# Attention in a two-layer trunk: the loop over heads turned into a loop over branches, four heads per value matmul

## The chip, the cores and the metric

The kernel runs on one core of a Trainium2 chip. The metric is the device time of one execution in microseconds (us), lower is better. A core has a tensor engine (PE), a vector engine (DVE), a scalar engine (ACT), GpSimd (POOL) and a sync engine (SP) that issues most loads. Each engine works through its own instructions strictly in the order in which they were queued when the program was built. PE writes only into PSUM banks of 128 partitions by 512 float32 values.

## The reference

Two layers, each of a mixer (three branches in parallel: this attention, and two recurrences), a cross attention and a gated feed-forward part, over 512 positions of width 1024. The change lies in the attention of the mixer. Eight query heads of 64 share two groups of keys and values (four heads to a group). Each head's output is a gated sum of three attentions: over compressed keys, over selected blocks, and over a causal window. With 512 positions there are 8 blocks, and all of them are selected, so the last two are plain causal softmax attentions over different keys and values.

```python
s = jnp.einsum('bgqhd,bgqnd->bgqhn', qb, kg).astype(F32) * scale
p = masked_softmax(s, mask)
return jnp.einsum('bgqhn,bgqnd->bgqhd', p.astype(vg.dtype), vg)
...
g = jax.nn.sigmoid(gate_logits.astype(F32)).reshape(B, S, G, HG, 3)
o = g[..., 0:1] * o_cmp + g[..., 1:2] * o_sel + g[..., 2:3] * o_win
```

## The kernel before

All weights are multiplied in a split form: `load_w` loads a float32 tile `wr`, ACT rounds it to `wh`, DVE subtracts to get `wl`, and three matmuls of 512 columns stand for one. A gate projection (`gate(b, n)`) is 24 such matmuls into one bank of the pool `pd`, followed by a multiplication on DVE and a tanh on ACT.

The attention (`nsa_attn`) takes the positions in four blocks `i` of 128 queries. Block `i` attends to `W = 128 (i+1)` keys, so the widths are 128, 256, 384 and 512. A block begins with the compressed branch for all eight heads: eight small matmuls against `kcT`, a chain of a dozen short DVE operations and one exponential, a transpose, and the tile `pc`. Then come 16 softmaxes (8 heads, two branches `br`). For one softmax PE writes the scores into a bank of the pool `pa` (two score matmuls and one that adds the causal mask, `negb`), DVE finds the row maximum (TENSOR_REDUCE) and scales it (a one-column TENSOR_TENSOR), ACT takes the exponential with its row sum (ACTIVATE and ACTIVATION_READ_ACCUMULATOR), which frees the bank. Four softmaxes make a group: one reciprocal of the four sums, one multiplication by the gate, four scalings (TENSOR_SCALAR, L1097), transposes on PE into the pool `pt`, copies from there to SBUF on ACT, and value matmuls from those copies.

Before, a group is one head index `j` with both key groups and both branches. Its output bank `po` comes from `pa`, and its value matmuls have 128 columns.

A scheduler orders each engine's instructions when the program is built: it may bring a later instruction ahead of an earlier one if its operands and its buffer are free by then. In source order the gate projections for the other two branches stand behind the attention, in `mixer`. The pools have these numbers of buffers:

```python
return pp.tile([P, T], F32, tag="pd", name=f"pd_{uid[0]}", bufs=3)
...
return pp.tile([P, T], F32, tag="pa", name=f"pa_{uid[0]}", bufs=2)
...
return pp.tile([P, T], F32, tag="pt", name=f"pt_{uid[0]}", bufs=3)
```

Of the kernel before, what the change touches and what calls it, by code (L numbers as in the profile page):

```python
# [13 lines left out]
AF = mybir.ActivationFunctionType  # L14
# [5 lines left out]
P = 128  # L20
# [68 lines left out]
TOK_VS, TOK_VW, TOK_HI, TOK_G, TOK_B, TOK_A = 0, 128, 256, 512, 536, 540  # L89
# [110 lines left out]
def tile_trunk(ctx, tc, a, out, dbg=None):  # L200
    nc = tc.nc
    dbg = dbg or {}
    V, S, G, TE = nc.vector, nc.scalar, nc.gpsimd, nc.tensor
# [7 lines left out]
    def tl(tag, bufs, shape=(P, T), dt=F32):  # L211
        uid[0] += 1
        return sb.tile(list(shape), dt, tag=tag, name=f"{tag}_{uid[0]}", bufs=bufs)

    def chain():
        return tl("chain", NCHAIN)

    def pd():
        uid[0] += 1
        return pp.tile([P, T], F32, tag="pd", name=f"pd_{uid[0]}", bufs=3)  # L220

    def pa():
        uid[0] += 1
        return pp.tile([P, T], F32, tag="pa", name=f"pa_{uid[0]}", bufs=2)

    def pt():
        uid[0] += 1
        return pp.tile([P, T], F32, tag="pt", name=f"pt_{uid[0]}", bufs=3)

    def small(n, dt=F32):  # L230
        if n <= 16:
            return tl("tiny", 40, (P, 16), dt)[:, :n]
        return tl("small", 10, (P, 64), dt)[:, :n]

    def mm(out_, lhsT, rhs, start=True, stop=True):
        TE.matmul(out_, lhsT, rhs, start=start, stop=stop, skip_group_check=True)  # L236
# [5 lines left out]
    def act(o, i, f=AF.Copy, **kw):  # L242
        S.activation(o, i, f, **kw)  # L243

    def tt(o, x, y, op, eng=None):
        (eng or V).tensor_tensor(o, x, y, op)  # L246

    def ts(o, x, s1, s2, op0, op1=None, eng=None):
        if op1 is None:
            (eng or V).tensor_scalar(o, x, s1, None, op0)  # L250
        else:
            (eng or V).tensor_scalar(o, x, s1, s2, op0, op1)
# [4 lines left out]
    MUL, ADD, SUB, MAX = ALU.mult, ALU.add, ALU.subtract, ALU.max  # L257

    def mark(name):
        if "mark" in dbg:  # L260
            dbg["mark"](name, nc)
# [7 lines left out]
    ident = cm[:, C_ID:C_ID + P]  # L269
# [185 lines left out]
    vcpad = [cst.tile([P, 4, 64], F32, name=f"vcpad{i}") for i in range(2)]  # L455
# [571 lines left out]
    def nsa_attn(l, tok, y, st):  # L1027
        KH, KL, QS, kcT, r8 = (st[k] for k in ("KH", "KL", "QS", "kcT", "r8"))
        mark("attn")
        gall = tl("gall", 1, (P, NT, 24))  # L1030
        act(gall, tok[:, :, TOK_G:TOK_G + 24], AF.Tanh, scale=0.5)
        ts(gall, gall, 0.5, 0.5, MUL, ADD)

        for i in range(NT):
            qs_ = slice(i * P, (i + 1) * P)
            sc = pa()
            for j in range(4):
                for g_ in range(2):
                    mm(sc[:, (4 * g_ + j) * 64:(4 * g_ + j + 1) * 64], QS[j, g_][:, qs_],
                       kcT[:, g_].rearrange("p a n -> p (a n)"))  # L1040
            e = tl("tg", NTG)[:, :256].rearrange("p (h n) -> p h n", h=8)
            m3 = cmpm[:, i:i + 1, :].to_broadcast([P, 8, 32])
            pen = tl("cmpn", 1, (P, 32))
            ts(pen, cmpm[:, i, :], -NEG, NEG, MUL, ADD)
            p3 = pen[:, None, :].to_broadcast([P, 8, 32])
            s4 = sc.rearrange("p (h a n) -> p h a n", a=2, n=32)
            tt(e, s4[:, :, 0], p3, ADD)
            tt(e, e, s4[:, :, 1], ADD)
            b8 = lambda t_, n_=32: t_.rearrange("p (h o) -> p h o", o=1).to_broadcast([P, 8, n_])
            tt(e, e, b8(r8[:, i]), MUL)  # L1050
            mx = small(8)
            V.tensor_reduce(mx, e, AX.X, MAX)
            tt(e, e, b8(mx), SUB)
            act(e, e, AF.Exp)
            tt(e, e, m3, MUL)
            dn = small(8)
            V.tensor_reduce(dn, e, AX.X, ADD)
            ts(dn, dn, 1e-30, None, MAX)
            V.reciprocal(dn, dn)
            g3 = gall[:, i, :].rearrange("p (h b) -> p h b", b=3)  # L1060
            cf = small(8)
            tt(cf, dn, g3[:, :, 0], MUL)
            tt(e, e, b8(cf), MUL)
            ps = pt()
            for g_ in range(2):
                TE.transpose(ps[:, g_ * P:(g_ + 1) * P], e[:, g_ * 4:g_ * 4 + 4, :].rearrange("p h n -> p (h n)"), ident)
            pc = tl("tg", NTG)
            act(pc[:, :256], ps[:, :256])

            for j in range(4):  # L1070
                hd = {}
                W = (i + 1) * P
                WM = max(W, 256)
                den = small(4)
                prs = []
                for g_ in range(2):
                    for br in range(2):
                        q_ = QS[j, g_][:, qs_]
                        ps = pa()
                        mm(ps[:, :WM], q_, KH[br, g_][:, :WM], stop=False)  # L1080
                        mm(ps[:, :WM], q_, KL[br, g_][:, :WM], start=False, stop=False)
                        mm(ps[:, i * P:W], identb, negb, start=False, stop=True)
                        nm = small(1)
                        V.tensor_reduce(nm, ps[:, :W], AX.X, MAX, negate=True)  # L1084
                        rc = r8[:, i, 4 * g_ + j:4 * g_ + j + 1]
                        tt(nm, nm, rc, MUL)
                        pr = chain()
                        act(pr[:, :W], ps[:, :W], AF.Exp, bias=nm, scale=rc, accum_out=den[:, 2 * g_ + br:2 * g_ + br + 1])
                        prs.append(pr)
                V.reciprocal(den, den)  # L1090
                g4 = gall[:, i, :].rearrange("p (g j b) -> p g j b", g=2, b=3)[:, :, j, 1:]
                tt(den.rearrange("p (g b) -> p g b", g=2), den.rearrange("p (g b) -> p g b", g=2), g4, MUL)
                for g_ in range(2):
                    for br in range(2):
                        x_ = 2 * g_ + br
                        pr = prs[x_]
                        ts(pr[:, :W], pr[:, :W], den[:, x_:x_ + 1], None, MUL)  # L1097
                        pst = pt()
                        for k in range(i + 1):
                            TE.transpose(pst[:, k * P:(k + 1) * P], pr[:, k * P:(k + 1) * P], ident)  # L1100
                        pT = chain()
                        act(pT[:, :W], pst[:, :W])
                        hd[g_, br] = pT
                po = pa()
                o_ = [po[g_ * 64:(g_ + 1) * 64, :P] for g_ in range(2)]
                for g_ in range(2):
                    mm(o_[g_], vcpad[g_][:, j, :], pc[:, g_ * P:(g_ + 1) * P], start=True, stop=False)
                for br, off in ((0, TOK_VS), (1, TOK_VW)):
                    for k in range(i + 1):
                        for g_ in range(2):  # L1110
                            mm(o_[g_], tok[:, k, off + g_ * 64:off + g_ * 64 + 64], hd[g_, br][:, k * P:(k + 1) * P],
                               start=False, stop=(br == 1 and k == i))
                act(y[j][:, qs_], po[:, :P])
                yield


    def mem_phase(norm):
# [90 lines left out]
    def mixer(l, norm):  # L1208
# [68 lines left out]
        for _ in nsa_attn(l, tok, ya, st):  # L1277
            pass
# [169 lines left out]
```

## Time and profile before

| what | value |
|---|---|
| median of 3 runs | 2110.07 us (2108.05 to 2112.93) |
| the profiled execution: span, which is all that its profile gives of its own time | 2108.7 us |
| PE matmuls, busy | 2057.5 us, 98% of the span |
| DVE busy | 1430.0 us, 68% |
| ACT busy | 951.3 us, 45% |
| POOL busy | 131.9 us, 6% |

Busy time is the time in which an engine has at least one instruction under way. A matmul's record lasts from its start until its results have landed, and the next one starts before that, so that PE can be busy all the time and still not be at its peak: the distance from start to start tells what a matmul costs. The attention of the first layer runs from 365.7 to 552.7 us of the span and that of the second from 1398.5 to 1586.1 us.

### The profile page before, as it was taken

Reading aid. Unit: us, or ns where it says so; the run is one execution under the profiler, and the core shown is the slowest. Engines: PE = TensorE matmul, PEld = TensorE weight load, DVE = VectorE, ACT = ScalarE, POOL = GpSimd, SP = SyncE. Lnnn points to the kernel's source line nnn. Section 1 sums busy time; section 2 is a strip of 40 time slices with the busy share of each in tenths; the row PEclk is TensorE's granted clock in tenths of the full one; section 3 lists DMA queues with packets and bytes.
Section 4 is the critical chain, followed back from the end, with each engine's and each line's share of the span. In section 5 each row is a group of like instructions: output and inputs, shape, how many; then the busy total and the mean of one; then the engine's idle time right before and its main releaser. Section 6 shows DMA issues by size and latency. Waiting matters only on the chain. (4 is left out here: it accounts for less than half of the span.)

```text
span 2108.7 us, 31046 instructions
## 1 busy us (share of the span) xinstructions
PE 2057.5 (98%) x11396; PEld 1610.2 (76%) x11400; DVE 1430.0 (68%) x3070; ACT 951.3 (45%) x1854; POOL 131.9 (6%) x120
## 2 busy tenths in 40 slices
PE   8999999999999999999999998999999999999999
PEld 7877677777786788888888776777778758888887
DVE  6764898666656887377548469975667577755773
ACT  6434444555545544244434344445554454433442
POOL 1000122000010100000000003110000110000000
PEclk9999999999999999999999999999999999999999
DMA  7332222111241233323432312121113413333333
GB/s 237 90 101 68 77 74 64 52 51 46 64 140 47 88 95 95 95 94 96 120 107 76 101 42 90 59 72 51 46 46 91 126 52 92 95 93 98 95 98 108
DMA packets 116809, 180.90 MB, mean 86 GB/s; under 512 B 19696, under 2 KB 37232, under 8 KB 116656
## 3 DMA queue, kind: packets, MB, share of 16 engines
q1 hardware_dynamic: 88992, 158.64, 25.1%
q10 hardware_dynamic: 27584, 19.97, 3.3%
q8 instruction: 90, 1.47, 0.3%
q14 instruction: 63, 0.52, 0.1%
q0 software_dynamic: 80, 0.29, 0.0%
HBM read 170.21 MB, written 8.65 MB: 85 GB/s over the span
## 5 line engine op out<-in xcount | busy, mean ns | idle before, releaser
L236 PE MATMUL pd<-act,wh 128*128 128x512 f32 x3008 | 985.4, 403 | 0.0
L243 ACT ACTIVATE wh<-wr 128x512 fp32r<-128x512 f32 (+2 forms) x586 | 365.5, 624 | 657.5 <-PE pd L236 566.3
L236 PEld LDWEIGHTS pd<-act,wh 128*128 128x128 f32 x3008 | 560.6, 189 | 128.4 <-issue 14.4
L236 PE MATMUL pd<-act,wl 128*128 128x512 f32 x1504 | 605.6, 403 | 1.4 <-DVE wl L246 1.4
L246 DVE TENSOR_TENSOR wl<-wr,wh 128x512 fp32r<-128x512 f32 (+2 forms) x586 | 406.7, 694 | 212.3 <-ACT wh L243 205.0
L236 PE MATMUL pd<-chain,wh 128*128 128x512 f32 x1344 | 426.7, 397 | 4.4 <-DVE gate L255 3.2
L236 PEld LDWEIGHTS pd<-act,wl 128*128 128x128 f32 x1504 | 284.3, 189 | 69.0 <-issue 6.1
L236 PEld LDWEIGHTS pd<-chain,wh 128*128 128x128 f32 x1344 | 251.0, 188 | 66.0 <-ACT chain L243 3.7
L236 PE MATMUL pd<-chain,wl 128*128 128x512 f32 x672 | 266.4, 396 | 0.3
L246 DVE TENSOR_TENSOR gate<-pd,rb 128x512 f32<-128x512 f32 x168 | 116.0, 691 | 102.8 <-PE pd L236 101.3
L236 PE MATMUL pa<-chain,chain 128*64 128x64 f32 (+7 forms) x1248 | 163.2, 296 | 2.3 <-ACT chain L243 1.0
L236 PEld LDWEIGHTS pd<-chain,wl 128*128 128x128 f32 x672 | 126.6, 188 | 30.3 <-DVE wl L246 1.1
L255 DVE SCALAR_TENSOR_TENSOR gate<-gate,vec,gate 128x511 f32<-128x511 f32 (+1 forms) x176 | 132.1, 751 | 21.5 <-ACT gate L243 18.3
L236 PEld LDWEIGHTS pa<-chain,chain 128*64 128x64 f32 (+3 forms) x1248 | 109.1, 163 | 45.5 <-issue 21.0
L1084 DVE TENSOR_REDUCE tiny<-pa 128x1 f32<-128x128 f32 (+3 forms) x128 | 61.1, 487 | 81.7 <-PE pa L236 81.3
L243 ACT ACTIVATE chain<-pa,tiny,r 128x128 f32<-128x128 f32 (+3 forms) x128 | 78.9, 617 | 60.7 <-DVE tiny L246 56.3
L246 POOL TENSOR_TENSOR chain<-chain,t 128x512 f32<-128x512 f32 x30 | 40.7, 1355 | 1014.7 <-ACT t L243 949.0
L243 ACT ACTIVATE chain<-pt 128x512 f32<-128x512 f32 (+3 forms) x156 | 61.1, 445 | 63.9 <-PE pt L1100 37.2
L243 ACT ACTIVATE gate<-gate,vec 128x512 f32<-128x512 f32 x88 | 63.8, 726 | 27.9 <-DVE gate L246 27.9
L236 PE MATMUL pa<-chain,tok 128*64 128x128 f32 x704 | 62.3, 282 | 0.0
L255 DVE SCALAR_TENSOR_TENSOR t<-t,gate 128x512 f32<-128x512 f32 x88 | 60.5, 688 | 2.0 <-ACT t L243 0.4
L246 POOL TENSOR_TENSOR tg<-tg,chain 128x256 f32<-128x256 f32 (+1 forms) x42 | 45.5, 1089 | 191.1 <-ACT tg L243 78.5
(238 smaller groups left out, 2001.5 us busy)
## 6 DMA issues: line engine op xcount, KB each, us to landing
wr<-in_w_fm SPq DMA_DIRECT2D x184, 256.0 KB, 2.7
wr<-in_w_up SPq DMA_DIRECT2D x176, 256.0 KB, 2.6
wr<-in_w_dn SPq DMA_DIRECT2D x64, 256.0 KB, 2.7
wr<-in_w_mix SPq DMA_DIRECT2D x32, 256.0 KB, 2.7
wr<-in_w_dn SPq DMA_DIRECT2D x32, 192.0 KB, 2.4
wr<-in_w_tk SPq DMA_DIRECT2D x16, 272.0 KB, 2.9
wr<-in_w_kv SPq DMA_DIRECT2D x16, 256.0 KB, 3.8
chain<-in_cmp_w SPq DMA_DIRECT2D x16, 256.0 KB, 4.1
```

Of the source, the lines that this page charges most:

```text
L236: TE.matmul(out_, lhsT, rhs, start=start, stop=stop, skip_group_check=True)
L243: S.activation(o, i, f, **kw)
L246: (eng or V).tensor_tensor(o, x, y, op)
L255: V.scalar_tensor_tensor(o, x, s, y, op0, op1)
L1084: V.tensor_reduce(nm, ps[:, :W], AX.X, MAX, negate=True)
```

## The change

The loop over heads `j` with both branches inside becomes a loop over branches `br`, then key groups `g_`, with the four heads inside. A group of four softmaxes is now one branch of one key group. For each key block `k` the four heads' transposes go side by side into one `pt` bank, one copy of 512 columns takes them to SBUF (`pT[g_, k]`), and one value matmul of 512 columns serves all four heads. The output bank `po` of a whole block, 512 columns wide, now comes from `pd`. It is written first by the eight value matmuls of the compressed branch, collects both branches, and is copied out at the end of the block by four copies, two on ACT and two on DVE.

```diff
+            W = (i + 1) * P
+            WM = max(W, 256)
+            po = pd()
+            o_ = [po[g_ * 64:(g_ + 1) * 64] for g_ in range(2)]
             for j in range(4):
-                hd = {}
-                W = (i + 1) * P
-                WM = max(W, 256)
-                den = small(4)
-                prs = []
                 for g_ in range(2):
-                    for br in range(2):
+                    mm(o_[g_][:, j * P:(j + 1) * P], vcpad[g_][:, j, :], pc[:, g_ * P:(g_ + 1) * P],
+                       start=(j == 0), stop=False)
+            g5 = gall[:, i, :].rearrange("p (g j b) -> p g j b", g=2, b=3)
+            for br, off in ((0, TOK_VS), (1, TOK_VW)):
+                pT = {}
+                for g_ in range(2):
+                    den = small(4)
+                    prs = []
+                    for j in range(4):
                         q_ = QS[j, g_][:, qs_]
...
-                V.reciprocal(den, den)
...
-                        for k in range(i + 1):
-                            TE.transpose(pst[:, k * P:(k + 1) * P], pr[:, k * P:(k + 1) * P], ident)
-                        pT = chain()
-                        act(pT[:, :W], pst[:, :W])
-                        hd[g_, br] = pT
-                po = pa()
...
-                act(y[j][:, qs_], po[:, :P])
+                    V.reciprocal(den, den)
+                    tt(den, den, g5[:, g_, :, 1 + br], MUL)
+                    for j in range(4):
+                        ts(prs[j][:, :W], prs[j][:, :W], den[:, j:j + 1], None, MUL)
+                    for k in range(i + 1):
+                        pst = pt()
+                        for j in range(4):
+                            TE.transpose(pst[:, j * P:(j + 1) * P], prs[j][:, k * P:(k + 1) * P], ident)
+                        pT[g_, k] = chain()
+                        act(pT[g_, k], pst)
+                for k in range(i + 1):
+                    for g_ in range(2):
+                        mm(o_[g_], tok[:, k, off + g_ * 64:off + g_ * 64 + 64], pT[g_, k],
+                           start=False, stop=(br == 1 and k == i))
                 yield
+            for j in range(4):
+                (S.copy if j % 2 else V.tensor_copy)(y[j][:, qs_], po[:, j * P:(j + 1) * P])
+            yield
```

The change also moves instructions on every engine. In the rows below `pd_5236` and the like are banks of `pd`, `act` and `wh`, `wl` the split activations and weights of the projections, `tg` is `pc`, and `chain` stands for queries, keys, probabilities and their transposes.

PE at the start of block 0 of the first layer, before:

```order
L236 MATMUL pa_3876<-chain_2583,chain_3724 128x256
L236 LDWEIGHTS identb
L236 MATMUL pa_3876<-negb,identb 128x128
L236 MATMUL pd_5236<-act_160,wh_5239 128x512
L236 MATMUL pd_5236<-act_161,wh_5239 128x512
L236 MATMUL pd_5236<-act_160,wl_5240 128x512
L236 MATMUL pd_5236<-act_202,wh_5239 128x512
L236 MATMUL pd_5236<-act_203,wh_5239 128x512
L236 MATMUL pd_5236<-act_202,wl_5240 128x512
L236 MATMUL pa_3885<-chain_2594,chain_3724 128x256
```

PE at the same place, with the change:

```order
L236 MATMUL pa_3885<-negb,identb 128x128
L236 MATMUL pa_3894<-chain_2582,chain_3730 128x256
L236 MATMUL pa_3894<-chain_2583,chain_3730 128x256
L236 LDWEIGHTS identb
L236 MATMUL pa_3894<-negb,identb 128x128
L1066 MATMUL pt_3870<-cm,tg_3852 128x128 x2
L236 MATMUL pa_3903<-chain_2582,chain_3736 128x256
L236 MATMUL pa_3903<-chain_2583,chain_3736 128x256
L236 LDWEIGHTS identb
L236 MATMUL pa_3903<-negb,identb 128x128
L236 MATMUL pd_3875<-tg_3873,vcpad_86 64x128
```

The projection matmuls into `pd` no longer stand between the scores. In the whole order of PE the first of them now stands in block 3, after its compressed value matmuls, and four projections (96 matmuls) stand in that block; the others follow the attention.

PE between two groups of block 1, with the change (`pa_4191` and `pa_4200` are the first two scores of the next group, `pa_4209` is its third; `pt_4176` and `pt_4183` are the two transpose banks of the group before):

```order
L236 MATMUL pa_4200<-negb,identb 128x128
L1104 MATMUL pt_4176<-cm,chain_4141 128x128
L1104 MATMUL pt_4183<-cm,chain_4141 128x128
L1104 MATMUL pt_4176<-cm,chain_4150 128x128
L1104 MATMUL pt_4183<-cm,chain_4150 128x128
L1104 MATMUL pt_4176<-cm,chain_4159 128x128
L1104 MATMUL pt_4183<-cm,chain_4159 128x128
L1104 MATMUL pt_4176<-cm,chain_4168 128x128
L1104 MATMUL pt_4183<-cm,chain_4168 128x128
L236 MATMUL pd_4124<-chain_4181,tok_533 64x512
L236 MATMUL pa_4209<-chain_2588,chain_3739 128x256
```

Two scores stand ahead of the transposes, and the third stands behind the transposes and behind a value matmul that needs a copy of them (`chain_4181`).

DVE at such a boundary in block 1, before (`pa_4251` is the next group's first score):

```order
L1090 RECIPROCAL tiny_4175<-tiny_4175 128x4
L246 TENSOR_TENSOR tiny_4175<-tiny_4175,gall_3840 128x4
L246 TENSOR_TENSOR wl_5458<-wr_5455,wh_5457 128x512
L250 TENSOR_SCALAR chain_4183<-chain_4183,tiny_4175 128x256
L250 TENSOR_SCALAR chain_4192<-chain_4192,tiny_4175 128x256
L250 TENSOR_SCALAR chain_4201<-chain_4201,tiny_4175 128x256
L250 TENSOR_SCALAR chain_4210<-chain_4210,tiny_4175 128x256
L1084 TENSOR_REDUCE tiny_4255<-pa_4251 128x1
```

DVE and then ACT at such a boundary in block 1, with the change (`pa_4252` is the first score of the group after, `pt_4176` and `pt_4183` hold the transposes of the group before, `pa_4191` and `pa_4200` are the scores of the next):

```order
L1091 TENSOR_REDUCE tiny_4256<-pa_4252 128x1
L1097 RECIPROCAL tiny_4190<-tiny_4190 128x4
L246 TENSOR_TENSOR tiny_4256<-tiny_4256,r_769_3697 128x1
L246 TENSOR_TENSOR tiny_4190<-tiny_4190,gall_3840 128x4
L250 TENSOR_SCALAR chain_4198<-chain_4198,tiny_4190 128x256
L250 TENSOR_SCALAR chain_4207<-chain_4207,tiny_4190 128x256
L250 TENSOR_SCALAR chain_4216<-chain_4216,tiny_4190 128x256
L250 TENSOR_SCALAR chain_4225<-chain_4225,tiny_4190 128x256
```

```order
L243 ACTIVATE chain_4168,tiny_4133<-pa_4161,tiny_4165,r_769_3697 128x256
L243 ACTIVATE chain_4181<-pt_4176 128x512
L243 ACTIVATE chain_4188<-pt_4183 128x512
L243 ACTIVATE chain_4198,tiny_4190<-pa_4191,tiny_4195,r_769_3697 128x256
L243 ACTIVATE chain_4207,tiny_4190<-pa_4200,tiny_4204,r_769_3697 128x256
```

On DVE the next group's first maximum has moved ahead of the reciprocal. On ACT the copies of a group's transposes stand ahead of the next group's first exponential.

## Rows read from the trace of the kernel before

**Rows 1.** The page: span, busy time of PE, its busy tenths and granted clock.

```profile
span 2108.7 us, 31046 instructions
...
PE 2057.5 (98%) x11396; PEld 1610.2 (76%) x11400; DVE 1430.0 (68%) x3070; ACT 951.3 (45%) x1854; POOL 131.9 (6%) x120
...
PEclk9999999999999999999999999999999999999999
```

**Rows 2.** Busy us (x instructions) by engine in both attentions; granted clock, DMA share, GB/s.

```profile
365.70:552.70 187.00, 187.00 (x1181) 138.06 (x1180) 117.00 (x343) 101.88 (x265) 0.00 (x0) 1.00 0.16 49
1398.50:1586.10 187.60, 187.30 (x1181) 138.00 (x1179) 117.03 (x339) 101.72 (x265) 0.00 (x0) 1.00 0.16 49
```

**Rows 3.** The same windows, instructions on pd alone; then 610 to 630 us.

```profile
365.70:552.70 187.00, 118.85 (x405) 71.68 (x405) 15.11 (x22) 0.00 (x0) 1.00 0.16 49
...
610.00:630.00 20.00, 20.00 (x88) 16.11 (x86) 2.77 (x4) 0.00 (x0) 1.00 0.50 150
```

**Rows 4.** Timeline of PE in block 2: start, duration, instruction.

```profile
457.48 1.62 PE L1100 MATMUL pt<-cm,chain 128*128 128x128 f32 x12
...
459.39 0.50 PE L236 MATMUL pd<-act,wh 128*128 128x512 f32 x1
459.82 1.52 PE L236 MATMUL pa<-chain,tok 128*64 128x128 f32 x22
461.28 0.62 PE L236 MATMUL pa<-chain,chain 128*128 128x384 f32 x2
```

**Rows 5.** Timeline of one softmax of block 3, 512 wide.

```profile
531.72 0.63 PE L236 MATMUL pa<-chain,chain 128*128 128x512 f32 x2
...
532.46 0.69 DVE L1084 TENSOR_REDUCE tiny<-pa 128x1 f32<-128x512 f32 x1 [0.91 <-PE pa L236]
...
533.43 0.78 ACT L243 ACTIVATE chain<-pa,tiny,r 128x512 f32<-128x512 f32 x1 [0.98 <-DVE tiny L246]
...
534.11 0.19 ACT L243 ACTIVATION_READ_ACCUMULATOR chain<-pa,tiny,r 128x1 f32 x1
```

**Rows 6.** Groups in the first attention by line and shape: busy us, mean ns.

```profile
L243 ACT ACTIVATE chain<-pa,tiny,r 128x512 f32<-128x512 f32 x16 | 12.5, 780 | 8.2 <-DVE tiny L246 7.1 <-DVE tiny L1291 1.0
...
L1084 DVE TENSOR_REDUCE tiny<-pa 128x1 f32<-128x512 f32 x16 | 10.7, 687 | 12.3 <-PE pa L236 12.3
...
L243 ACT ACTIVATE chain<-pa,tiny,r 128x128 f32<-128x128 f32 x16 | 7.3, 457 | 6.0 <-DVE tiny L246 4.9 <-PE pa L236 1.0
...
L250 DVE TENSOR_SCALAR chain<-chain,tiny 128x512 f32<-128x512 f32 x16 | 6.7, 480 | 0.1
...
L1084 DVE TENSOR_REDUCE tiny<-pa 128x1 f32<-128x128 f32 x16 | 4.5, 287 | 6.7 <-PE pa L236 6.5
...
L250 DVE TENSOR_SCALAR chain<-chain,tiny 128x128 f32<-128x128 f32 x16 | 3.6, 281 | 0.1
```

**Rows 7.** Timeline of DVE, then of ACT, at the end of a group of block 3.

```profile
534.86 0.17 DVE L1090 RECIPROCAL tiny<-tiny 128x4 f32<-128x4 f32 x1
...
535.14 0.69 DVE L246 TENSOR_TENSOR wl<-wr,wh 128x512 fp32r<-128x512 f32 x1
535.75 1.67 DVE L250 TENSOR_SCALAR chain<-chain,tiny 128x512 f32<-128x512 f32 x4
...
537.13 2.06 ACT L243 ACTIVATE chain<-pt 128x512 f32<-128x512 f32 x4 [1.52 <-PE pt L1100]
```

**Rows 8.** Timeline of DVE at the head of block 3: the compressed branch.

```profile
497.17 0.42 DVE L1052 TENSOR_REDUCE tiny<-tg 128x8 f32<-128x256 f32 x1
...
499.98 0.68 DVE L1084 TENSOR_REDUCE tiny<-pa 128x1 f32<-128x512 f32 x1
```

**Rows 9.** Timeline of PE in the cross attention: float32 matmuls of 512 columns.

```profile
1716.22 1.88 PE L236 MATMUL pa<-chain,chain 128*128 128x512 f32 x4
```

**Rows 10.** Windows in that cross attention, columns as in rows 2.

```profile
1698.80:1702.20 3.40, 2.09 (x8) 0.96 (x7) 3.36 (x17) 2.25 (x7) 0.00 (x0) 0.99 0.27 77
1702.20:1705.60 3.40, 3.40 (x5) 1.32 (x5) 0.09 (x1) 0.00 (x1) 0.00 (x0) 0.50 0.00 0
```

More of the change, by code (lines that the diff above doesn't have):

```diff
@@ L1087, in nsa_attn @@
                         pr = chain()
-                        act(pr[:, :W], ps[:, :W], AF.Exp, bias=nm, scale=rc, accum_out=den[:, 2 * g_ + br:2 * g_ + br + 1])
+                        act(pr[:, :W], ps[:, :W], AF.Exp, bias=nm, scale=rc, accum_out=den[:, j:j + 1])
                         prs.append(pr)
-                V.reciprocal(den, den)
-                g4 = gall[:, i, :].rearrange("p (g j b) -> p g j b", g=2, b=3)[:, :, j, 1:]
-                tt(den.rearrange("p (g b) -> p g b", g=2), den.rearrange("p (g b) -> p g b", g=2), g4, MUL)
@@ L1093, in nsa_attn @@
[L1093 to L1097, printed above, removed]
-                        pst = pt()
-                        for k in range(i + 1):
-                            TE.transpose(pst[:, k * P:(k + 1) * P], pr[:, k * P:(k + 1) * P], ident)
-                        pT = chain()
-                        act(pT[:, :W], pst[:, :W])
-                        hd[g_, br] = pT
@@ L1104, in nsa_attn @@
-                po = pa()
[L1105 to L1112, printed above, removed]
```

## The prediction

> **What bounds the kernel now.** I read the page first. PE is busy 98% of the span, its granted clock is full in every slice [rows 1]; no other engine comes near. Then the windows of the two attentions: PE is busy 187.0 of 187.0 us and 187.3 of 187.6, while DVE works 117 and ACT 102 [rows 2]. The attention alone could not do that. The windows cut to the `pd` pool show why: 405 projection matmuls run inside each attention [rows 3]. Where nothing but projections runs, 88 take 20 us, 0.227 us each [rows 3], so they are 92 of the 187 us. They fill every moment in which a softmax waits for DVE or ACT. So a softmax's latency costs nothing now, and the question for the change is whether that cover stays.
>
> **What the change does to the cover.** `po` moves from `pa` to `pd`, which has three banks, and is held for a whole block. Blocks 0, 1 and 2 claim all three in turn, and the projections come behind them in source order. The order of PE shows the result: no projection matmul in blocks 0 to 2, 96 in block 3, the rest behind the attention. PE takes its queue in order, so no run can bring them forward. Of the 405, 309 move behind, where they cost 309 x 0.227 = 70 us per layer. With X for the attention's own time, a layer goes from 187 to X + 70: the change is even at X = 117.
>
> **X, from one group.** Everything now hangs on two `pa` banks and on the orders shown. All durations are of 512 columns first, then reduced for narrower blocks.
>
> A score takes 2.58 us from its first matmul (531.72) until the exponential and its sum are done (534.11 + 0.19) and the bank is free [rows 5]. A block of 128 keys saves 0.40 on the maximum (687 to 287 ns) and 0.32 on the exponential (780 to 457) [rows 6], and 0.23 because its two score matmuls are half as wide: 1.63. The widths between lie evenly between (scores are never narrower than 256): 1.87 and 2.22.
>
> The period of a group, for widths 512 / 384 / 256 / 128:
> - ACT copies the last group's transposes first, as its order shows: four copies in 2.06 us [rows 7], 0.5 each, one per key block: 2.0 / 1.5 / 1.0 / 0.5.
> - Then the first exponential, 0.87 until its bank is free (533.43 to 534.30) [rows 5]: 0.87 / 0.76 / 0.65 / 0.55.
> - The third score needs that bank; it takes a full 2.58 / 2.22 / 1.87 / 1.63.
> - The next group's first score takes the bank that this frees, and its maximum now stands ahead of the reciprocal on DVE: 0.74 to the maximum and 0.69 for it [rows 5], 1.43 / 1.18 / 0.93 / 0.80. The fourth softmax ends beside it.
> - Reciprocal to the end of the fourth scaling: 534.86 to 537.42, less the 0.61 of a foreign `wl` between [rows 7], 1.95; each scaling falls from 480 to 281 ns [rows 6]: 1.95 / 1.68 / 1.42 / 1.15.
> - The last transposes, 0.12 each (12 in 1.62 us [rows 4]), and their landing: 0.7 / 0.55 / 0.45 / 0.3.
>
> The sums are 9.5 / 7.9 / 6.3 / 4.9 us. On top comes a new wait: the value matmuls stand ahead of the third score on PE and wait for ACT's copies; behind them wait that score, and for it DVE and ACT. A 512-column float32 matmul is two instructions of 0.43 to 0.47 us (four in 1.88 [rows 9]). No row shows such a pair on two 64-column halves of the array. The 128-column ones do run side by side: 22 in 1.52 us, 0.07 each [rows 4], against 0.12 for a full-width transpose. So I take pairs that overlap, n value matmuls in (n+1) x 0.43, begun 0.65 after the first copy. Of each two groups one has 1 of them, the other 7 / 5 / 3 / 1. Against the copies and the first exponential this delays the third score by 0.6 / 0.5 / 0.35 / 0.45 on average. The other bound is no overlap: 20 pairs a layer at 0.86 more, 17 us a layer if all of it shows.
>
> Four groups a block make 27 us for 256, 34 for 384 and 21.5 for 128. Block 3 would be 40, but there PE's own work is more: 16 x 0.5 of scores, 64 transposes at 0.12, some 8 of value matmuls and 96 projections at 0.227, together 45. Each block also has a head. DVE's compressed chain takes 2.8 us from the row maximum to the first score's maximum [rows 8], and some 1.0 for the three operations before it. DVE's two output copies stand within it and wait for the last value matmuls. I put a head at 5 us, 3 to 6: 20 in all. X = 21.5 + 27 + 34 + 45 + 20 = 147.
>
> **What costs nothing.** Transposes (160 a layer), exponentials, maxima and reciprocals stay in number. The copies from `pt` move the same columns in 40 instead of 64 pieces. The output copies stay 16 a layer, half of them now on DVE. Value matmuls go from 0.07 x 320 = 22 us to 20 x 0.86 = 17, which is worth nothing while PE waits. The weight loads of the moved projections go later on SP; PE waits for none of them now and has 70 us of dense work to hide them in.
>
> **The sum.** 147 + 70 - 187 = +30.5 us a layer, +61 in two: 2108.7 + 61 = 2170. The span is all that the profile gives of its own time, and the median of the runs is 1.4 above it, so I predict 2171 us. A difference within 0.2%, 4 us, would be no change for this measurement.
>
> **The rivals.**
> *The bare blocks fall to half clock.* In the cross attention, PE busy 2.09 of 3.40 us while it waited for a softmax was followed by 3.40 us at 0.50 [rows 10], 1.2 instead of 2.4 GHz. Blocks 0 to 2 would keep PE about half busy. Their PE work is 15 of scores, 96 transposes at 0.12, 10 of value matmuls and 3 compressed, 39 us; at half clock it is 39 more, three quarters of it on the chain: +29 a layer, 2229. Against it: no slice of the page, 53 us each, shows a lower tenth [rows 1]. The Trainium skill, "TensorE: Matmul & The Clock Gate", section "Why this matters for your kernels", warns against idle gaps between bursts for this reason; the rows above agree with it.
>
> *Groups overlap, and attention beats its break-even.* If the chain at a group's end hid behind the next scores, only the two banks would set the pace: 8 x (1.63 + 1.87 + 2.22) = 46, 45 for block 3 and 3 a head: X = 103, 14 below even, 2108.7 - 28 + 1.4 = 2082. Faster. It decides wherever X falls under 117. Against it: ACT's and DVE's orders put the copies and the maximum where I counted them.
>
> *PE stays full and gains from fewer changes of kind.* Before a run of value matmuls a projection takes 0.43 us (459.39 to 459.82) instead of 0.227, with about 0.1 behind it [rows 4]: 0.3 a run. The order has 43 such runs a layer before and 20 now: 23 x 0.3 x 2 = 14 us, 2096. It needs projections between the softmaxes, and there are none in three blocks. The Trainium skill, "TensorEngine Tiling (Array Packing)", section "Tiling Modes", states that a change of the tiling mode drains the engine; by that rule alone the change gains, and the price of the switch in the rows agrees.
>
> *Nothing changes:* X lands at 117 by gains and losses that cancel, 2110.
>
> **How the numbers follow.** The forecast has 0.62, with its own range 2135 to 2210: heads of 3 us and hidden value waits below, unpaired value matmuls above. Half clock has 0.2, overlap 0.08, the fuller PE 0.04, no change 0.06. From 2105 to 2235 I leave out the two faster cases and the upper end of the half-clock one, under 2 in 10. Faster is 0.08 + 0.04 = 0.12; of the no-change case 0.05 lies within 0.2%; slower is the rest, 0.83.
>
> **What would show it.** In the profile after: an attention of 130 to 165 us without projections in its first three blocks, and PE idle for some 60 us of it; the waits of PE on ACT copies and of ACT on transposes, small today, among the longest; groups at 5 to 10 us; behind the attention some 70 us of dense projections at 0.227. A pair of 512-column value matmuls at 1.7 us would refute the overlap, granted clocks of 0.5 in the blocks would speak for half clock, and PE still full there would refute the step on the cover. The prediction is wrong if X is under 120.

## The result, and the profile after

The changed kernel takes 2244.09 us in the median (2242.49 to 2246.03) against 2109.06 for the kernel before beside it, a ratio of 1.0633 [1.0619, 1.0648]. Slower was right; 135 us is more than twice the 61 that the sum gave, and beyond the range's upper end of 2235.

The page of the changed kernel: span, busy time by engine, PE's busy tenths, granted clock.

```profile
span 2244.1 us, 30044 instructions
...
PE 2116.2 (94%) x10916; PEld 1625.9 (72%) x10920; DVE 1437.4 (64%) x3086; ACT 941.4 (42%) x1790; POOL 134.1 (6%) x120
...
PE   8999897779999999999999999977899999999999
...
PEclk9999998589999999999999999967999999999999
```

The span is 135.4 us longer than in [rows 1], and two places carry the mark: slices 7 to 9 and 27 to 29, counted from 1, the two attentions, where PE is no longer full and the clock falls to 0.5 to 0.8 of full speed (in the last of these slices it is full again). In [rows 1] every digit of the clock is a 9.

Windows of the changed kernel: blocks 0 to 3 of the first attention, the stretch behind it, and the whole second attention. Busy us (x instructions) of PE, PEld, DVE, ACT and POOL, then granted clock, DMA share, GB/s.

```profile
367.40:402.80 35.40, 23.97 (x94) 14.49 (x92) 15.06 (x70) 10.63 (x37) 0.00 (x0) 0.62 0.04 14
402.80:444.70 41.90, 31.38 (x114) 18.30 (x115) 18.02 (x70) 14.49 (x44) 0.00 (x0) 0.58 0.00 1
444.70:489.20 44.50, 32.02 (x139) 19.60 (x139) 20.59 (x70) 17.96 (x48) 0.00 (x0) 0.81 0.00 1
489.20:550.60 61.40, 58.74 (x289) 36.99 (x290) 33.30 (x90) 31.26 (x69) 0.00 (x0) 0.97 0.11 35
550.60:625.00 74.40, 73.85 (x312) 57.25 (x311) 34.87 (x55) 23.72 (x41) 0.00 (x0) 1.00 0.28 85
1467.10:1650.00 182.90, 144.92 (x635) 88.39 (x634) 87.07 (x296) 74.28 (x196) 0.00 (x0) 0.79 0.05 15
```

An attention takes 183 us, practically what it took before (187 in [rows 2]), but it does so with 635 matmul instructions instead of 1181, and the 74 us behind it are full of the projections that were pushed out. X, put at 147, was 183. That alone is 72 us in two layers, and with the forecast's 61 makes 133 of the 135. The miss is therefore X, 36 us a layer; all other terms together leave some 2 us of the 135.

The longest waits of blocks 0 to 2 (us in total, times, longest):

```profile
DVE tiny L1091 <- PE pa L236: 55.3, 25, 5.4
ACT chain L243 <- PE pt L1104: 33.1, 11, 4.0
ACT chain L243 <- DVE tiny L246: 29.6, 14, 3.4
PEld pa L236 <- ACT chain L243: 21.7, 19, 1.7
PE pa L236 <- ACT chain L243: 13.5, 14, 1.6
...
PE pd L236 <- ACT chain L243: 5.6, 11, 0.7
```

The same of the kernel before, blocks 0 to 2:

```profile
DVE tiny L1084 <- PE pa L236: 28.4, 19, 3.5
...
ACT chain L243 <- PE pt L1100: 11.5, 12, 2.0
```

The prediction named two waits. ACT's for the transposes came, 33.1 us where it was 11.5. PE's for ACT's copies, ahead of the value matmuls, did not grow long: 5.6 us. Longer is another wait of PE for ACT, 13.5 us: an exponential must read a bank of `pa` before the next score can have it. The longest, DVE's for scores, was not named. It was the longest before, too.

PE in block 1, partly and then wholly at half clock (first four rows), and in the window of block 3 at full clock (the twelve transposes are the last of block 2):

```profile
419.73 1.48 PE L1104 MATMUL pt<-cm,chain 128*128 128x128 f32 x8 [0.23 <-DVE chain L250]
421.68 1.97 PE L236 MATMUL pd<-chain,tok 128*64 128x512 f32 x2 [0.47 <-ACT chain L243]
...
428.08 1.97 PE L1104 MATMUL pt<-cm,chain 128*128 128x128 f32 x8 [0.23 <-DVE chain L250]
...
437.92 1.97 PE L1104 MATMUL pt<-cm,chain 128*128 128x128 f32 x8 [0.64 <-DVE chain L250]
...
491.09 1.53 PE L1104 MATMUL pt<-cm,chain 128*128 128x128 f32 x12 [0.23 <-DVE chain L250]
...
510.62 1.07 PE L236 MATMUL pd<-chain,tok 128*64 128x512 f32 x2
...
522.25 3.65 PE L236 MATMUL pd<-chain,tok 128*64 128x512 f32 x14
```

Eight transposes take up to 1.97 us in block 1; twelve take 1.53 at full clock. A single value matmul takes 1.97 and 1.07. Groups of block 1 follow each other at 8.35 and 9.84 us (419.73, 428.08, 437.92), where the sum had 6.3 and some 0.4 for the value matmuls.

### The profile page after: what moved, and what is told of

Same layout as the page of the kernel before. It is cut to its first block, busy times and chain, and to the rows that moved or that the text cites. A ratio compares the mean times of both kernels' runs of the same rounds, so it can differ in the third digit from the quotient of the medians.

```text
span 2244.1 us, 30044 instructions
## 1 busy us (share of the span) xinstructions
PE 2116.2 (94%) x10916; PEld 1625.9 (72%) x10920; DVE 1437.4 (64%) x3086; ACT 941.4 (42%) x1790; POOL 134.1 (6%) x120
## 5 line engine op out<-in xcount | busy, mean ns | idle before, releaser
L236 PE MATMUL pd<-act,wh 128*128 128x512 f32 x3008 | 971.4, 400 | 0.2
L236 PE MATMUL pa<-chain,chain 128*64 128x64 f32 (+7 forms) x1248 | 178.6, 310 | 29.6 <-ACT chain L243 25.4
L236 PEld LDWEIGHTS pa<-chain,chain 128*64 128x64 f32 (+3 forms) x1248 | 114.6, 171 | 96.1 <-ACT chain L243 50.0
L243 ACT ACTIVATE chain<-pt 128x512 f32<-128x512 f32 (+1 forms) x108 | 55.8, 566 | 120.2 <-PE pt L1104 94.1
L236 PE MATMUL pd<-chain,tok 128*64 128x512 f32 x160 | 72.0, 749 | 11.2 <-ACT chain L243 11.2
L1104 PE MATMUL pt<-cm,chain 128*128 128x128 f32 x320 | 61.0, 346 | 9.4 <-DVE chain L250 9.4
```

The costliest lines, as they stand in the source:

```text
L1104: TE.transpose(pst[:, j * P:(j + 1) * P], prs[j][:, k * P:(k + 1) * P], ident)
```

## Experiments

**The bank that `po` comes from.** Two runs turn the one line each way. In the first, the changed kernel's `po` gets a pool of its own with one bank, paid for with one of the three banks of `pt`; a control gives the kernel before two banks of `pt`.

```diff
-        return pp.tile([P, T], F32, tag="pt", name=f"pt_{uid[0]}", bufs=3)
+        return pp.tile([P, T], F32, tag="pt", name=f"pt_{uid[0]}", bufs=2)
...
+        return pp.tile([P, T], F32, tag="po", name=f"po_{uid[0]}", bufs=1)
...
-            po = pd()
+            po = pob()
```

> The changed kernel with its output bank in a pool of its own (one bank, taken from the transposes' pool, which goes from 3 to 2). In the order of PE 77, 83, 102 and 113 projection matmuls are back in the four blocks. If the loss of cover is the cause: each attention takes 170 to 190 us with PE full and the clock at 1.00, and the whole 2080 to 2120 us. If the new grouping (wider value matmuls, copies ahead of exponentials) is slow by itself: above 2180 us.

> Control: the kernel before with 2 transpose banks instead of 3. Both theories: within 0.5% of the kernel before, 2100 to 2120 us, so that the bank taken in the run with the own bank has no price of its own. Above 2120 us, the third transpose bank is worth something.

Measured: 2100.29 us against 2110.75, ratio 0.9958 [0.9942, 0.9974]; the control 1.0002 [0.9991, 1.0014]. The four blocks of the first attention, columns as above:

```profile
364.10:395.90 31.80, 31.80 (x170) 22.12 (x168) 20.50 (x79) 15.12 (x45) 0.00 (x0) 1.00 0.19 57
395.90:433.20 37.30, 37.20 (x198) 25.33 (x197) 24.34 (x80) 20.76 (x54) 0.00 (x0) 1.00 0.17 50
433.20:480.60 47.40, 47.21 (x241) 31.55 (x241) 30.63 (x88) 25.33 (x59) 0.00 (x0) 1.00 0.15 45
480.60:541.10 60.50, 60.48 (x308) 38.53 (x306) 38.98 (x100) 32.50 (x71) 0.00 (x0) 1.00 0.16 49
```

PE is full again and the clock is 1.00 in every block. The grouping, the wide value matmul and the orders on DVE and ACT are all still those of the change; with its own bank it is 10 us faster than the kernel before. A third bank of `pt` was worth nothing in the kernel before.

In the second, the kernel before keeps its loop over heads and only takes its `po` from `pd`:

```diff
-                po = pa()
+                po = pd()
```

> One part alone: the kernel before, its grouping kept, only the output bank of each head taken from the projections' pool. In the order of PE 0, 0, 0 and 34 projection matmuls stand in the four blocks. If the loss of cover is the cause: slower than before by 80 to 180 us, 2190 to 2290, with half clock in the first blocks. If the grouping is the cause: 2105 to 2120 us.

Measured: 2241.96 us, 1.0624 [1.0603, 1.0645]: as large a loss, from one word. Its page shows the same two dips, and behind it stand the windows of its first attention, of blocks 0 to 2 alone, and of the projections behind:

```profile
span 2240.4 us, 31075 instructions
...
PEclk9999997689999999999999999967999999999999
```

```profile
366.50:531.70 165.20, 134.87 (x812) 96.68 (x810) 81.38 (x286) 78.15 (x222) 0.00 (x0) 0.75 0.03 7
...
366.50:480.40 113.90, 90.00 (x475) 62.81 (x473) 53.25 (x206) 49.22 (x157) 0.00 (x0) 0.67 0.02 5
...
531.70:620.00 88.30, 87.74 (x372) 68.72 (x372) 39.38 (x60) 27.43 (x46) 0.00 (x0) 1.00 0.31 90
```

That the two losses are so nearly equal is chance. The attention is 18 us shorter than with the change, because fewer projections, 34 instead of 96 by the order of PE, stand in its block 3, and because its blocks 0 to 2 take 113.9 us at a clock of 0.67 instead of 121.8 at 0.68; the stretch behind it is 14 us longer. So without cover the old grouping, with an output bank for each head, is the faster one, by 8 us in these three blocks.

**How the pool shuts the projections out.** The prediction said that blocks 0, 1 and 2 hold all three banks. Then a fourth bank would let a projection in. This run has four banks of `pd` (and two of `pt`).

```diff
-        return pp.tile([P, T], F32, tag="pd", name=f"pd_{uid[0]}", bufs=3)
+        return pp.tile([P, T], F32, tag="pd", name=f"pd_{uid[0]}", bufs=4)
```

> The changed kernel with four banks for the projections and the output, two for transposes. If the number of banks decided (blocks 0 to 2 claim all three): a fourth bank would let projections into the blocks, and the time would fall below 2200 us. If the order of claims in one pool decides (a projection's bank is claimed behind that of block 3, however many there are): no projection in blocks 0 to 2, 2235 to 2250 us. The order of PE shows 0, 0, 0 and 99 projection matmuls.

Measured, in a single run: 2256.31 us, 6 above what was expected, and the order of PE still has no projection in blocks 0 to 2. So it is not the count of banks. What fits is that banks of one pool are given out in the order of the source: the first projection stands behind four `po` of the attention and gets no bank before the fourth has its own, in block 3. That is tested from the other side by leaving the pools alone and writing eight gate projections between the attention's steps:

```diff
+        queue += [(b, n) for b in "ba" for n in range(KD)]
+        early = NGATE - KD
         for _ in nsa_attn(l, tok, ya, st):
-            pass
+            if early:
+                gate(*queue.pop(0))
+                early -= 1
...
-        queue += [(b, n) for b in "ba" for n in range(KD)]
-        for n in range(NGATE - KD):
-            gate(*queue.pop(0))
```

> The changed kernel, pools untouched, but eight gate projections written between the groups in the source instead of behind the attention, so that they claim their banks ahead of the later blocks' outputs. The order of PE shows 72, 72, 48 and 105 projection matmuls in the blocks. If cover is all: clock near 1.00, the attention's blocks near 30, 37, 40 and 60 us, the whole 2105 to 2140 us. If a bank held for a whole block is what costs: above 2180 us.

Measured: 2166.02 us, 1.0265 [1.0245, 1.0286]. More than half of the loss is back, though less than expected. Its first three blocks:

```profile
367.80:406.70 38.90, 34.22 (x172) 23.44 (x171) 21.66 (x85) 16.36 (x49) 0.00 (x0) 0.91 0.14 47
406.70:447.90 41.20, 36.60 (x191) 26.11 (x189) 23.24 (x77) 19.95 (x51) 0.00 (x0) 0.92 0.12 39
447.90:492.30 44.40, 37.06 (x180) 23.35 (x178) 24.69 (x72) 21.62 (x53) 0.00 (x0) 0.92 0.10 30
```

```profile
PE pt L1066 <- DVE tg L246: 10.1, 3, 3.4
```

The second fence is a row of its waits in these blocks. Projections now run in them, but not under the heads of the blocks: PE waits there three times for DVE's compressed chain, 10.1 us. How the rest of the loss divides between these waits, the clock and the bank that `po` still takes was not measured.

**What the half clock costs.** PE is given useless bf16 matmuls to do while it waits. First six per group into the bank of the first transposes:

```diff
                         pst = pt()
+                        if i < 3 and k == 0:
+                            for _ in range(6):
+                                mm(pst, identb, negt)
```

> The changed kernel with six useless bf16 matmuls of 512 columns per group in blocks 0 to 2, written into a transpose bank before the transposes overwrite it. They keep PE busier and compute nothing that is used. If the half clock makes the difference between the forecast and the measured time: granted clock near 1.00 in these blocks, 2170 to 2200 us. If the chains of DVE and ACT are longer than I counted: 2230 us or more at a higher clock.

Measured: 2228.05 us, 1.0558 [1.0535, 1.0582], between the two expectations, because parts of the blocks still ran at half clock. Blocks 0 to 2 of the changed kernel's first layer took 121.8 us at an average clock of 0.68; here they took

```profile
365.70:478.10 112.40, 84.65 (x418) 48.74 (x416) 52.66 (x210) 42.85 (x127) 0.00 (x0) 0.86 0.02 5
```

Then five behind every second score, into a bank `dm` of their own, which is again one of the three of `pt`:

```diff
+                        if i < 3 and j % 2:
+                            for _ in range(5):
+                                mm(dm, identb, negt)
```

> The changed kernel with five useless bf16 matmuls of 512 columns behind every second score of blocks 0 to 2, into a bank of their own (taken from the transposes), spread more evenly than in the run before it. They compute nothing that is used. If the half clock accounts for the 24 us by which blocks 0 to 2 exceed my count: granted clock 1.00 there, the three blocks fall from 122 to about 100 us a layer, and the whole to 2190 to 2215 us. If the chains on DVE and ACT are longer than I counted, clock or not: the blocks stay above 112 us at clock 1.00, the whole above 2225 us.

Measured: 2230.52 us, 1.0574 [1.0547, 1.0602]. The total misleads. Windows of blocks 0 to 2 of either layer, first for `dm` alone (PE busy, then clock, DMA share, GB/s), then for block 0 of either layer with all engines:

```profile
365.00:467.80 102.80, 58.60 (x217) 1.00 0.02 6
1441.90:1569.00 127.10, 0.00 (x0) 0.61 0.01 5
```

```profile
1441.90:1478.00 36.10, 24.83 (x94) 15.22 (x92) 15.13 (x67) 10.72 (x37) 0.00 (x0) 0.55 0.05 15
...
365.00:394.00 29.00, 28.81 (x161) 15.20 (x160) 14.81 (x70) 10.37 (x37) 0.00 (x0) 1.00 0.05 19
```

The useless matmuls depend on nothing in a layer, and the scheduler ran those of the second in the first. So one execution holds both cases: 102.8 us with them at a clock of 1.00, and 127.1 without at 0.61. (In the changed kernel itself the second layer's three blocks took 121.1 us.) To have both layers alike, the third run puts one matmul on the score's own operands ahead of eight useless ones:

```diff
+                        if i < 3 and j % 2:
+                            mm(dm[:, :WM], q_, KH[br, g_][:, :WM])
+                            for _ in range(8):
+                                mm(dm, identb, negt)
```

> Nothing of the computation is changed: behind every second score of blocks 0 to 2 PE gets one more matmul on that score's operands, so that it can't be brought forward into the other layer, and eight useless bf16 matmuls, all into a bank that nothing reads. If the half clock is a price of its own, both attentions now run at full clock, some 163 us each instead of 183 (layer 1 of the run before took 163.5), and the time is 2244 - 2 x 19 = 2206 us, 2195 to 2220. If the half clock only accompanies the waits, the granted clock rises and the time stays at 2235 to 2260.

Measured: 2214.18 us, 1.0500 [1.0482, 1.0517]. Blocks 0 to 3 of the first layer, blocks 0 to 2 of the second, and the transposes of block 1:

```profile
364.70:394.00 29.30, 29.22 (x168) 16.28 (x167) 16.23 (x76) 10.97 (x38) 0.00 (x0) 1.00 0.05 18
394.00:427.80 33.80, 33.63 (x192) 18.54 (x191) 16.52 (x65) 13.90 (x42) 0.00 (x0) 1.00 0.00 1
427.80:468.80 41.00, 38.46 (x205) 19.83 (x203) 20.56 (x70) 18.40 (x49) 0.00 (x0) 1.00 0.00 1
468.80:531.20 62.40, 59.90 (x292) 37.12 (x292) 33.32 (x89) 31.56 (x70) 0.00 (x0) 0.97 0.11 34
1447.60:1552.60 105.00, 101.91 (x562) 54.90 (x560) 53.63 (x206) 43.44 (x127) 0.00 (x0) 1.00 0.02 6
```

```profile
407.61 0.44 PE L1113 MATMUL pt<-cm,chain 128*128 128x128 f32 x2
...
414.36 1.22 PE L1113 MATMUL pt<-cm,chain 128*128 128x128 f32 x8
...
422.09 1.09 PE L1113 MATMUL pt<-cm,chain 128*128 128x128 f32 x8
```

With more work on PE the kernel is 30 us faster than the changed one (2244.09 - 2214.18). Blocks 0 to 2 go from 121.8 to 104.1 us, and the groups of block 1 follow at 6.75 and 7.73 instead of 8.35 and 9.84. The half clock has a price of its own, at least 15 us a layer, since the useless matmuls may themselves stand in the way. A changed order is hardly the reason: of ACT's 127 instructions in these three blocks, 125 stand, by their names and shapes, in the same sequence with and without them. DVE's wait for scores is shorter, but stays the longest:

```profile
DVE tiny L1100 <- PE pa L240: 40.1, 19, 4.5
```

So of the 55.3 us of the changed kernel most is not PE's lower clock.

**What the wide value matmul is worth.** The version with its own bank, its value matmuls cut back into four of 128 columns:

```diff
-                        mm(o_[g_], tok[:, k, off + g_ * 64:off + g_ * 64 + 64], pT[g_, k],
-                           start=False, stop=(br == 1 and k == i))
+                        for j in range(4):
+                            mm(o_[g_][:, j * P:(j + 1) * P], tok[:, k, off + g_ * 64:off + g_ * 64 + 64],
+                               pT[g_, k][:, j * P:(j + 1) * P], start=False, stop=(br == 1 and k == i))
```

> The version with the output's own bank, and with the value matmuls cut back to 128 columns, four for one. With PE full again the wide matmul would be worth (4 x 0.218 - 0.86) per pair, next to nothing, if only columns count: 2097 to 2106 us. If the wide matmul is what makes the own-bank version faster than the kernel before: 2108 us or more.

Measured: 2102.59 us, 0.9965 [0.9954, 0.9977], beside 0.9958 [0.9942, 0.9974] with the wide ones. The intervals lie over each other: the width itself could not be told from nothing, and the gain stays without it. It comes from what both versions share: the grouping, and an output bank that is no longer one of the two of `pa`. No run tells these two apart; the kernel before with a bank of its own for `po` was not run.

## Why the prediction failed in size, step by step

**Cover lost: right, and it is the whole sign.** The projections left blocks 0 to 2, ran behind the attention for some 70 us, and the two runs on the bank turn the loss off (2100) and on (2242). The explanation beside it, that three blocks claim three banks in turn, fell with the run with four banks. What stands in its place, banks given out in source order, fits both runs on it and the kernel before with `po` from `pd`, where no projection starts ahead of block 3 either, but it was not seen at work and stays open.

**X = 147: the failed step, 36 us a layer short.** Of the signs that the prediction set, an attention of at most 165 us and some 60 us of idle PE did not come (183, and 37 by the windows), and the sign of its half-clock rival did (granted 0.58 to 0.81). The 36 us split by the third run with useless matmuls, which has both layers at full clock:

- *Half clock, some 17 us a layer.* The forecast took the rows' full clock for blocks whose PE would be half busy, and left the fall to a rival at 0.2. In the result blocks 0 to 2 were granted 0.62, 0.58 and 0.81 and took 121.8 us; at full clock they took 104.1, and 105.0 in the second layer. The reason given against the rival, that no slice of before showed a lower tenth, was none: in those slices the projections kept PE full. The small place in the cross attention where they did not [rows 10] was the evidence. The rival had the mechanism, and its 29 us a layer was too high for another reason than its price. It took the three blocks to be at half clock throughout, 97.5 + 29 = 126.5 us, which is 0.23 us lost for each us at half clock. If each granted clock is a mix of full and half, 76%, 84% and 38% of the three blocks were at half clock, an estimated 79 of the 121.8 us, and 17.7 lost (121.8 - 104.1) in 79 is 0.22. The share of the time was too high; whether three quarters of the slowed work lies on the chain was not measured by itself. The Trainium skill, "TensorE: Matmul & The Clock Gate", section "Why this matters for your kernels", warns of idle gaps between bursts; this case agrees: filling PE's waits was worth 30 us for the kernel.
- *Block 3, 12 us.* 50 were forecast with its head, 61.4 and 62.4 measured. PE is busy 58.74 of 61.40 there, so its own work, put at 45, was undercounted. Two rows and a pair show where:

```profile
493.15 2.79 PE L236 MATMUL pd<-chain,tok 128*64 128x512 f32 x10
...
500.06 1.97 PE L236 MATMUL pd<-tg,vcpad 128*64 128x128 f32 x16
...
505.45 0.48 PE L236 MATMUL pd<-act,wh 128*128 128x512 f32 x1
505.76 0.63 PE L236 MATMUL pa<-chain,chain 128*128 128x512 f32 x2
```

  Five value matmuls of block 2 run in block 3 (2.79), and so do the twelve transposes shown above (1.53); the compressed value matmuls (1.97, still at half clock) were not in its sum, and a projection ahead of another kind takes 0.31 (505.45 to 505.76) instead of 0.227. The rest is not split further. [rows 2, 3] could have warned: 187 us of full PE less 92 of projections leaves 95 for everything else, while the counts in the prediction, 39 for blocks 0 to 2 and 23 for block 3, come to 62.
- *Blocks 0 to 2 at full clock, 7 us.* 104.1 with the useless matmuls against 26.5 + 32 + 39 = 97.5. The chain of a group was sized nearly right: 6.75 and 7.73 in block 1 against some 6.7.

**Overlap of value matmuls: right.** 7 of them (14 instructions) take 3.65 us, where (n+1) x 0.43 gives 3.44 and no overlap 6.0; 1 takes 1.07 against 0.86.

**What was put at nothing.** Behind the attention PE is busy 73.85 of 74.4 us, so the later weight loads are hidden, as was said. The other entries of that list were not measured one by one.

**The fuller PE with fewer changes of kind,** a rival at 2096, is where the version with its own bank comes out: 2100.3, a gain of 10 where 14 were worked out. In its trace PE makes 20 runs of 64-column matmuls in an attention, with the narrow value matmuls 23 and 22, and 43 in the kernel before. That a gain of 8 stays with the narrow ones speaks for the runs between changes as the source and not the width, but does not show it, since `po` also leaves `pa` in both. The Trainium skill, "TensorEngine Tiling (Array Packing)", section "Tiling Modes", says that a change of mode drains the engine; the 10 us for 23 fewer runs a layer, 0.22 us a run where the rows gave 0.3, are in line with it.

## What to carry to other kernels

Before a long-held buffer is moved to another pool, look at who else draws on that pool behind it in the source: here one word, `pd()` for `pa()`, cost 6% in the kernel before, and with a bank of its own for `po` the change was a gain of 0.4%. When filler work leaves a stretch, take the stretch's matmuls at the lower clock as well, unless something still keeps PE full; a full clock in the trace of before says only that it was full before. And check a sum of one engine's work against a window in which that engine is full: what is left after the known part is the price that the sum has to give.

## What the runs showed of the hardware

- Blocks in which PE was busy 23.97 of 35.40 and 31.38 of 41.90 us were granted 0.62 and 0.58, so that a stretch that waits becomes slower still. The same blocks filled with useless matmuls ran at 1.00 and in 29.3 and 33.8 us: work that nobody reads made the kernel 30 us faster.
- At half clock a run of eight transposes takes 1.97 us; at full clock twelve take 1.53. The same holds for value matmuls: one in 1.97 and in 1.07 us.
